# The first pass of a SwiGLU output product with eight fast pairs in place of six

## The chip, the cores and the metric

The kernel runs on one core of one Trainium2 chip. The metric is the device time of one execution in microseconds. All inputs are in device memory when it starts, and the output is written back there.

A core has TensorE (matrix products, into PSUM), VectorE ("DVE" in the profile), ScalarE ("ACT"), GpSimd ("POOL") and SyncE ("SP"), which here mostly issues transfers. Each runs its own list of instructions in order, and they wait for each other by semaphores.

## The reference

One layer of a decoder for 256 rows of 2048 columns, in float32:

```python
h = rms_norm(x, norm1_gain) * (1 + scale1) + shift1
x = x + gate1 * mixing_sublayer(h, ...)          # attention branches, w_out
h = rms_norm(x, norm2_gain) * (1 + scale2) + shift2
gate, up = jnp.split(h @ w_ffn_in, 2, axis=-1)   # 2048 -> 2 x 5632
x = x + gate2 * ((silu(gate) * up) @ w_ffn_out)  # 5632 -> 2048
```

The shift, scale and gate rows come from a product of silu(c) with w_ada. The change lies in the last product, (256 x 5632) @ (5632 x 2048).

## The kernel before

**Products in three parts.** TensorE multiplies a reduced float type (fp32r). So each factor is split in a high part (a cast on ScalarE) and a low part (VectorE subtracts the high part from the number), and `mm3` (L173 to L175) adds high x high, high x low and low x high: three matmuls of a 128 x 128 left factor with 512 weight columns. Weights come as 128 x 2 x 512 tiles ("raw"), transferred on SP's queue (L216), are cast (L236) and split (L222 in `sub`) into a hi and a lo tile, here called a room.

**The last product.** Its left factor is `act`, 11 units of 512 columns that the FFN before it made, each a hi and a lo tile. In chunks of 128 rows of the weights there are 44, so 22 pairs. It is done in two passes, over 1024 output columns each, by `fast_products`; pass one follows the order `OUT_A`, pass two `OUT_B`. An entry is a pair number and whether the pair is done by seven products.

**A pair.** The two chunks of a pair, the two column halves (512 each) and the two row tiles form a 2 x 2 by 2 x 2 block product. A plain pair takes eight `mm3`, 24 matmuls. A fast pair takes seven, 21 matmuls, by a scheme of Strassen's kind; it needs sums and differences of both factors. Those of the weights are made for every fast pair in `load_pair`: it splits r0 (1024 columns a partition), makes `ta` and `tb` (four subtractions of 512 columns in the rooms AR0 and A8, `OUT_TAGS`), and splits half of r1, `ta` and `tb`. The subtractions of all pairs of a pass are chained in their order (`chain`). Those of the left factor are made once for a unit, which is two pairs, in `sums_of_unit`: the sum of hi and lo (L1555) in AR0, four sums of 256 columns (L207) in A8, a cast (L1559) and the low part (L1560). Four units have them: 4, 5, 6 and 3 (`OUT_UNITS`), for the pairs 8 to 13, 6 and 7. A room given out by a tag belongs to one tile after the other in the order of the program: the next tile's writer waits for the last reader of the one before.

**Order of the work.** A planner lays out each engine's list. `load_pair` runs with raised priority, `LOOK` = 3 pairs ahead of the pair multiplied; the weights go round five rooms (four of a pool and X1 with X2) and, in pass one, six raw tiles (four and OD, KD); in pass two there are four. Other work fills in: at each position of the pass one step of the second gate row's sums is issued (`ada_mac`, L421; eight are left for this pass, each not before the split of the pair loaded last), and `hooks` names positions at which more is issued: the sums of units 4, 5 and 6 at positions 2, 4 and 6, the return of two column blocks of the residual at 15 and 16, and the gate row's finish at 19, 20 and 21 (`parts_of_gate2`, `rows_of_gate2`, L1577 to L1587), where position 21 also has the sums of the fourth unit, unit 3. After the last fast pair the four PSUM banks of shared products are put together (L312 to L316) and added into the output banks (`merge`, L272), for one row tile before position 20 and for the other before 21. Then `add_out` multiplies by the gate and adds to the residual (L1539, L1541).

In `OUT_A` before, positions 0 to 7 are plain, then fast pairs 8 to 13 alternate with plain pairs 14 to 19 (positions 8 to 19), and 20 and 21 are plain.

Of the kernel before, what the change touches and what calls it, by code (L numbers as in the profile page):

```python
# [11 lines left out]
F32R = mybir.dt.float32r  # L12
# [5 lines left out]
P = 128  # L18
# [27 lines left out]

FAST = range(2, 11)
OUT_UNITS = (4, 5, 6, 3)
OUT_A = tuple((p, 0) for p in range(8)) + tuple(x for i in range(6) for x in ((8 + i, 1), (14 + i, 0))) + ((20, 0), (21, 0))
OUT_B = ((0, 0), (1, 0)) + tuple(x for a, b in zip((8, 9, 10, 11, 12, 13, 6, 7), (2, 3, 4, 5, 14, 15, 16, 17)) for x in ((a, 1), (b, 0)))  # L50
PAIRS = ((0, 0), (1, 0), (5, 1), (2, 0), (6, 1), (7, 1), (3, 0), (4, 0))
PAIRS_4 = ((0, 0), (1, 0), (4, 1), (5, 1), (2, 0), (6, 1), (7, 1), (3, 0))
# [28 lines left out]
def trunk(ctx: ExitStack, tc: tile.TileContext, I, out):  # L81
# [12 lines left out]
    def nm(base):  # L94
        uid[0] += 1
        return f"{base}_{uid[0]}"

    def S(tag, shape, dtype=F32):
        return slot.tile(shape, dtype, tag=tag, name=nm(tag))
# [10 lines left out]
    def misc_bank(shape):  # L110
        return psm.tile(shape, F32, tag="misc", name=nm("misc"))
# [10 lines left out]
    state = {"rate": 0.0}  # L122
# [78 lines left out]
    def sums_of(sf, h, a, b):  # L201

        (a0, b0), (a1, b1) = ((x[:, a, :], x[:, b, :]) for x in h)
        for dst, x, y, op in (
            (0, a1, b1, ALU.add), (2, a0, a1, ALU.subtract), (1, sf[:, 0], a0, ALU.subtract), (3, b0, sf[:, 1], ALU.subtract)
        ):
            nc.vector.tensor_tensor(sf[:, dst], x, y, op=op)  # L207
# [1037 lines left out]
    for j in range(2):  # L1245
        hi = S(gtag[0][j], [P, 4, T], F32R)
        lo = S(gtag[1][j], [P, 4, T], F32R)
# [145 lines left out]
    def bring_back(n, tag):  # L1393
        x2[n] = S(tag, [P, NT, NB])
        nc.sync.dma_start(x2[n], x2_away[n])
# [87 lines left out]
    for i in range(NFF):  # L1483
# [30 lines left out]
        if ftags[2 * i] == ftags[2 * i + 1]:  # L1514
            hl = S(ftags[2 * i], [P, 2, 4, T], F32R)
            hi, lo = hl[:, 0], hl[:, 1]
        else:
            hi, lo = (S(tag, [P, 4, T], F32R) for tag in ftags[2 * i : 2 * i + 2])
# [17 lines left out]
    def add_out(n, t, ps, a=0, end=NB, base=0, store=True):  # L1536

        tmp = scr([P, end - a])
        nc.vector.tensor_mul(tmp, gate2[n][:, a:end], ps[:, a - base : end - base])  # L1539
        xr = x2[n][:, t, a:end]  # L1540
        nc.vector.tensor_add(xr, xr, tmp)  # L1541
        if store:
            nc.sync.dma_start(out[t * P : (t + 1) * P, n * NB + a : n * NB + end], xr)
# [7 lines left out]
    def sums_of_unit(n):  # L1551

        e = OUT_UNITS[n]
        full = S(OUT_TAGS[0], [P, 4, T])
        nc.vector.tensor_tensor(full, act[e][0].bitcast(F32), act[e][1].bitcast(F32), op=ALU.add)  # L1555
        sf = S(OUT_TAGS[1], [P, 4, 2, P])
        sums_of(sf, [full[:, :, t * P : (t + 1) * P] for t in range(NT)], slice(0, 4, 2), slice(1, 4, 2))
        hi, lo = (S(tag, [P, 4, 2, P], F32R) for tag in (("H2", "H3"), ("H4", "H5"), ("H6", "H7"), ("OD", "KD"))[n])
        nc.scalar.copy(hi, sf)  # L1559
        nc.vector.tensor_tensor(lo, sf, hi.bitcast(F32), op=ALU.subtract)  # L1560
        for m in range(2):
            out_sums[2 * e + m] = [(hi[:, j, m, :], lo[:, j, m, :]) for j in range(4)]


    state["more_rooms"] = (("X1", "X2"),)
    state["more_raws"] = ("OD", "KD")
    state["chain"] = None
    hooks = {at: (lambda n=n: sums_of_unit(n)) for n, at in enumerate((2, 4, 6))}
    state["rate"] = RATE_OUT
    ring["tags"] = ("OS1", "OS2")  # L1570
    bg.append(gate2_end())
# [3 lines left out]
    def parts_of_gate2(j):  # L1575
        hi, lo = (S(tag, [P, 2 * NB], F32R) for tag in OUT_TAGS)
        nc.scalar.copy(hi, state["gate2"][j])  # L1577
        nc.vector.tensor_tensor(lo, state["gate2"][j], hi.bitcast(F32), op=ALU.subtract)
        parts.append((hi, lo))

    def rows_of_gate2(j):
        for c in (slice(0, NB), slice(NB, 2 * NB)):
            ps = misc_bank([P, NB])
            with tc.issue_after(state["mm"].ins):
                for i, x in enumerate(parts[j]):
                    nc.tensor.matmul(ps, ones_r, x[:, c], start=i == 0, stop=i == 1)
            nc.scalar.copy(state["gate2"][j][:, c], ps)  # L1587

    def both(j):
        rows_of_gate2(j)  # L1590
        parts_of_gate2(j + 1)

    for n in range(2):
        hooks[15 + n] = lambda n=n: bring_back(n, ("OS1", "OS2")[n])
    behind = 1 + max(n for n, (_, fast) in enumerate(OUT_A) if fast)
    assert behind + 2 < len(OUT_A)
    hooks[behind] = lambda: parts_of_gate2(0)
    hooks[behind + 1] = lambda: both(0)
    hooks[behind + 2] = lambda: (rows_of_gate2(1), sums_of_unit(3))
    o = fast_products(w_fo, 0, NB, OUT_A, act_at, out_sums, acc_bank, misc_bank, OUT_TAGS, hooks)  # L1600
    gate2 = [a[:, c : c + NB] for a in state["gate2"] for c in (0, NB)]
    with prio():
        for n in range(2):
            for t in range(NT):
                add_out(n, t, o[n][t])
    state["more_raws"] = ()
    o = fast_products(w_fo, 2 * NB, 3 * NB, OUT_B, act_at, out_sums, misc_bank, acc_bank, OUT_TAGS, more=True)
    for n in (2, 3):
        bring_back(n, f"H{n}")
# [6 lines left out]
    n, pss = 3, o[1]  # L1616
# [42 lines left out]
```

## Time and profile before

| | |
|---|---|
| median of 3 runs | 1576.88 us (1576.4 to 1577.58) |
| the profiled execution | 1578.32 us |
| its span | 1576.5 us |
| matmuls on TensorE | 7186 |
| granted clock of TensorE | 1.000 |
| first pass of the last product on TensorE | 1339.58 to 1457.98 us of the span |

The profile has one execution. A span begins with the first instruction and ends with the last. "Busy" is the time in which an engine executes; a TensorE that is busy may still be paced by pipelining, so its starts are the better measure. In a timeline a line gives start, duration, engine, source line, operation, written and read tiles by name (numbers left out: AR for AR0, X for X0, X1 or X2), count, and in brackets idle time before it with what ended it. An instruction's duration overlaps the next by some 0.09 us on VectorE, so prices are taken from start to start.

### The profile page before, as it was taken

What the parts mean: (1) busy time and instruction counts of PE and PEld (TensorE: products, weight loads), DVE (VectorE), ACT (ScalarE), POOL (GpSimd) and SP (SyncE); (2) the same over time, 40 slices, a digit from 0 to 9 for tenths busy, and PEclk for the clock granted to TensorE, in tenths of its full rate; (3) what the DMA queues carried; (4) which work ended last, traced back from release to release, by engine and by line L of the source; (5) the groups of instructions that cost most, each with busy time, mean ns of one, the idle gap of its engine ahead of it and who ended that gap; (6) DMA issues with size and microseconds to landing.
All of it is one profiled execution on the core that took longest, in us unless ns stands there. A gap on an engine that the chain in (4) does not pass through costs nothing.

```text
span 1576.5 us, 20259 instructions
## 1 busy us (share of the span) xinstructions
PE 1563.9 (99%) x7186; PEld 1293.5 (82%) x7186; DVE 1394.4 (88%) x1704; ACT 876.0 (56%) x1215; POOL 12.3 (1%) x24
## 2 busy tenths in 40 slices
PE   8999999999999999999999999999999999999998
PEld 7878888888888788888888888888888888888887
DVE  6889996888889899987987888999999999899896
ACT  5654448875765545344444645556555555455553
POOL 1000000000000000000000000000000000000000
PEclk9999999999999999999999999999999999999999
DMA  9999987677787788879897886565566566876664
GB/s 333 362 325 322 333 309 239 216 240 228 236 294 262 259 268 298 298 260 317 305 328 256 299 305 216 187 213 188 200 202 212 174 201 235 287 228 201 222 208 140
DMA packets 196317, 402.26 MB, mean 255 GB/s; under 512 B 13102, under 2 KB 28116, under 8 KB 196216
## 3 DMA queue, kind: packets, MB, share of 16 engines
q1 hardware_dynamic: 194952, 397.75, 74.7%
q0 software_dynamic: 1088, 3.16, 0.5%
q8 instruction: 56, 0.92, 0.2%
q14 instruction: 45, 0.37, 0.1%
q10 hardware_dynamic: 176, 0.07, 0.0%
HBM read 395.68 MB, written 5.24 MB: 254 GB/s over the span
## 4 chain that ended last, share of the span: by engine, by line
PE 89%; DVE 4%; DMA 3%; ACT 2%; issue 1%; SPq 0%; ACTq 0%; DVEq 0%
PE acc L175 20%; PE acc L174 20%; PE acc L173 20%; PE misc L174 7%; PE misc L173 7%; PE misc L175 7%; DMA raw<-w_br_gla 1%; DVE wlo L222 1%; DVE wlo L166 1%; DMA T<-w_in 1%; PE acc L576 1%; PE misc L945 1%; DVE A L222 1%; DMA raw<-w_in 1%; ACT whi L165 1%
## 5 line engine op out<-in xcount | busy, mean ns | idle before, releaser
L165 ACT CAST whi<-raw 128x1024 fp32r<-128x1024 f32 (+1 forms) x277 | 278.8, 1012 | 290.6 <-PE acc L175 186.1
L166 DVE TENSOR_TENSOR wlo<-raw,whi 128x1024 fp32r<-128x1024 f32 (+1 forms) x277 | 321.8, 1171 | 94.4 <-ACT whi L165 93.3
L173 PE MATMUL acc<-whi,H 128*128 128x512 f32 x997 | 390.4, 392 | 1.0 <-ACT H L588 0.8
L174 PE MATMUL acc<-wlo,H 128*128 128x512 f32 x997 | 388.9, 390 | 0.8 <-DVE wlo L166 0.7
L175 PE MATMUL acc<-whi,H 128*128 128x512 f32 x997 | 388.8, 391 | 0.5 <-DVE H L595 0.4
L175 PEld LDWEIGHTS acc<-whi,H 128*128 128x128 f32 x997 | 187.0, 188 | 40.2 <-DVE H L595 1.4
L173 PEld LDWEIGHTS acc<-whi,H 128*128 128x128 f32 x997 | 187.2, 188 | 39.7 <-ACT H L588 1.3
L174 PEld LDWEIGHTS acc<-wlo,H 128*128 128x128 f32 x997 | 187.4, 188 | 39.1 <-DVE wlo L166 1.7
L236 ACT CAST whi<-raw 128x1024 fp32r<-128x1024 f32 (+1 forms) x130 | 125.4, 976 | 68.7 <-PE acc L175 31.8
L222 DVE TENSOR_TENSOR wlo<-raw,whi 128x1024 fp32r<-128x1024 f32 (+1 forms) x130 | 144.0, 1125 | 14.2 <-ACT whi L236 12.8
L175 PE MATMUL acc<-whi,A 128*128 128x512 f32 x221 | 86.1, 389 | 0.0
L174 PE MATMUL acc<-wlo,A 128*128 128x512 f32 x210 | 81.8, 390 | 0.4 <-DVE wlo L166 0.4
L173 PE MATMUL acc<-whi,A 128*128 128x512 f32 x210 | 82.0, 390 | 0.0
L174 PE MATMUL misc<-wlo,H 128*128 128x512 f32 (+1 forms) x190 | 73.6, 387 | 1.6 <-DVE wlo L222 1.6
L173 PE MATMUL misc<-whi,H 128*128 128x512 f32 (+1 forms) x190 | 73.6, 387 | 0.0
L175 PE MATMUL misc<-whi,H 128*128 128x512 f32 (+1 forms) x190 | 73.5, 387 | 0.0
L222 DVE TENSOR_TENSOR A<-raw,A 128x1024 fp32r<-128x1024 f32 (+2 forms) x54 | 53.9, 1002 | 0.8 <-ACT A L236 0.4
L421 DVE SCALAR_TENSOR_TENSOR ada<-AR,csil,ada 128x1024 f32<-128x1024 f32 x39 | 49.6, 1280 | 5.1 <-DMA AR<-w_ada 5.1
L175 PEld LDWEIGHTS acc<-whi,A 128*128 128x128 f32 x221 | 41.5, 188 | 8.6
L236 ACT CAST A<-raw 128x1024 fp32r<-128x1024 f32 (+1 forms) x36 | 35.9, 1003 | 20.4 <-PE acc L175 8.9
L174 PEld LDWEIGHTS acc<-wlo,A 128*128 128x128 f32 x210 | 39.4, 188 | 8.9 <-DVE wlo L166 0.8
L173 PEld LDWEIGHTS acc<-whi,A 128*128 128x128 f32 x210 | 39.4, 188 | 8.1
(682 smaller groups left out, 3039.0 us busy)
## 6 DMA issues: line engine op xcount, KB each, us to landing
raw<-w_in SPq DMA_DIRECT2D x192, 512.0 KB, 5.0
raw<-w_ffn_in SPq DMA_DIRECT2D x135, 512.0 KB, 4.5
raw<-w_ffn_out SPq DMA_DIRECT2D x73, 512.0 KB, 5.2
AR<-w_ada SPq DMA_DIRECT2D x62, 512.0 KB, 4.9
raw<-w_out SPq DMA_DIRECT2D x32, 512.0 KB, 5.1
OS<-w_ada SPq DMA_DIRECT2D x24, 512.0 KB, 5.9
KD<-w_ada SPq DMA_DIRECT2D x22, 512.0 KB, 5.1
AR<-w_ffn_in SPq DMA_DIRECT2D x22, 512.0 KB, 4.3
```

Source lines behind the costliest of these rows:

```text
L165: state["cast"] = nc.scalar.copy(hi[:, :n, :], raw[:, :n, :])
L166: state["split"] = nc.vector.tensor_tensor(lo[:, :n, :], raw[:, :n, :], hi[:, :n, :].bitcast(F32), op=ALU.subtract)
L173: nc.tensor.matmul(ps, lh, rh, start=start, stop=False, skip_group_check=seeded)
L174: nc.tensor.matmul(ps, lh, rl, start=False, stop=False, skip_group_check=seeded)
L175: state["mm"] = nc.tensor.matmul(ps, ll, rh, start=False, stop=stop, skip_group_check=seeded)
L222: done = nc.vector.tensor_tensor(dst, x, y, op=ALU.subtract)
L236: nc.scalar.copy(hi[:, :n, :], src)
L421: nc.vector.scalar_tensor_tensor(acc, raw, c, acc, op0=ALU.mult, op1=ALU.add)
L576: state["warm"] = nc.tensor.matmul(ps, ones_r, wide, start=True, stop=True)
L945: nc.tensor.matmul(ps[:n, t * N_GLA + h, :].rearrange("p (s l) -> p s l", l=L), at(f, h, t)[:, :n], odd(at(f, h, t)), start=True, stop=True,)
```

## The change

`OUT_A` gets eight fast pairs: positions 0 to 3 are plain pairs 0 to 3, then fast pairs 8 to 13, 6, 7 alternate with plain pairs 4, 5, 14 to 19 (positions 4 to 19, fast ones at the even positions), and 20 and 21 are as before. The sums of the four units are issued at positions 1, 5, 9 and 13; those of the fourth go to X0 and KD, so KD is no raw tile any more. The raw tile OD stays one in the second pass.

```diff
-OUT_A = tuple((p, 0) for p in range(8)) + tuple(x for i in range(6) for x in ((8 + i, 1), (14 + i, 0))) + ((20, 0), (21, 0))
+OUT_A = tuple((p, 0) for p in range(4)) + tuple(
+    x for a, b in zip((8, 9, 10, 11, 12, 13, 6, 7), (4, 5, 14, 15, 16, 17, 18, 19)) for x in ((a, 1), (b, 0))
+) + ((20, 0), (21, 0))
...
     def sums_of_unit(n):
...
-        hi, lo = (S(tag, [P, 4, 2, P], F32R) for tag in (("H2", "H3"), ("H4", "H5"), ("H6", "H7"), ("OD", "KD"))[n])
+        hi, lo = (S(tag, [P, 4, 2, P], F32R) for tag in (("H2", "H3"), ("H4", "H5"), ("H6", "H7"), ("X0", "KD"))[n])
...
-    state["more_raws"] = ("OD", "KD")
+    state["more_raws"] = ("OD",)
     state["chain"] = None
-    hooks = {at: (lambda n=n: sums_of_unit(n)) for n, at in enumerate((2, 4, 6))}
+    hooks = {at: (lambda n=n: sums_of_unit(n)) for n, at in enumerate((1, 5, 9, 13))}
...
-    hooks[behind + 2] = lambda: (rows_of_gate2(1), sums_of_unit(3))
+    hooks[behind + 2] = lambda: rows_of_gate2(1)
     o = fast_products(w_fo, 0, NB, OUT_A, act_at, out_sums, acc_bank, misc_bank, OUT_TAGS, hooks)
...
-    state["more_raws"] = ()
     o = fast_products(w_fo, 2 * NB, 3 * NB, OUT_B, act_at, out_sums, misc_bank, acc_bank, OUT_TAGS, more=True)
```

## The prediction

> **What bounds the kernel now.** I read the page first, then the last 240 us in windows, then VectorE's and TensorE's timelines there. The profiled execution took 1578.32 us, its span is 1576.5 us, so 1.8 us lie around it; it stands 1.4 us above the median of the runs, 1576.88 us. I work out a difference inside the span and add it to the median. 0.2%, about what a measurement of this kernel can tell from no change, is 3.15 us.
>
> ```profile
> span 1576.5 us, 20259 instructions
> PE 1563.9 (99%) x7186; PEld 1293.5 (82%) x7186; DVE 1394.4 (88%) x1704; ACT 876.0 (56%) x1215; POOL 12.3 (1%) x24
> ```
>
> ```profile
> 1360.00:1370.00 10.00, 10.00 (x46) 8.29 (x45) 7.68 (x7) 3.97 (x4) 0.00 (x0) 1.00 0.91 313
> ...
> 1400.00:1410.00 10.00, 10.00 (x46) 8.29 (x45) 9.80 (x13) 5.79 (x6) 0.00 (x0) 1.00 0.79 261
> 1410.00:1420.00 10.00, 10.00 (x45) 8.29 (x45) 8.85 (x11) 5.79 (x6) 0.00 (x0) 1.00 0.64 204
> ...
> 1510.00:1520.00 10.00, 10.00 (x46) 8.29 (x45) 9.15 (x11) 5.78 (x6) 0.00 (x0) 1.00 0.65 212
> ```
>
> The columns after the stretch are TensorE, weight loads, VectorE (DVE), ScalarE, GpSimd, granted clock, DMA share, GB/s. TensorE is fed without a hole; VectorE is close behind, at 9.80 us of 10 where seven-product and plain pairs alternate. So TensorE sets the time, but VectorE has little left.
>
> **What the change takes from TensorE.** TensorE's timeline gives starts:
>
> ```profile
> 1362.23 0.39 PE L173 MATMUL acc<-whi,A 128*128 128x512 f32 x1
> ...
> 1434.99 0.39 PE L173 MATMUL misc<-whi,T 128*128 128x512 f32 x1
> ...
> 1439.76 0.39 PE L173 MATMUL acc<-whi,AR 128*128 128x512 f32 x1
> ...
> 1445.20 0.39 PE L1586 MATMUL misc<-AR,ones_r 128*128 128x512 f32 x1
> ...
> 1446.13 0.39 PE L173 MATMUL acc<-X,H 128*128 128x512 f32 x1
> ```
>
> Position 18 of the pass, a pair by seven products, runs from 1434.99 to 1439.76: 4.77 us for 21 matmuls. Position 19, plain, runs to 1445.20: 5.44 us for 24. The change makes two more pairs fast: 2 x 0.67 = 1.34 us off TensorE. An alternation of both is 10.21 us. Position 4 starts at 1362.23, in the changed kernel too, since positions 0 to 3 are plain in both.
>
> **What it puts on VectorE.** One alternation, and what else runs there:
>
> ```profile
> 1415.92 1.22 DVE L222 TENSOR_TENSOR wlo<-KD,whi 128x1024 fp32r<-128x1024 f32 x1 [0.92 <-ACT whi L236]
> 1417.29 2.36 DVE L222 TENSOR_TENSOR wlo<-raw,whi 128x1024 fp32r<-128x1024 f32 x2
> 1419.57 0.68 DVE L222 TENSOR_TENSOR AR<-raw,raw 128x512 f32<-128x512 f32 x1
> 1420.17 0.68 DVE L222 TENSOR_TENSOR AR<-raw 128x512 f32<-128x512 f32 x1
> 1420.77 0.68 DVE L222 TENSOR_TENSOR wlo<-raw,whi 128x512 fp32r<-128x512 f32 x1
> 1421.37 0.68 DVE L222 TENSOR_TENSOR A<-raw,AR 128x512 f32<-128x512 f32 x1
> 1422.09 0.69 DVE L222 TENSOR_TENSOR A<-raw,A 128x512 f32<-128x512 f32 x1
> 1422.70 1.22 DVE L222 TENSOR_TENSOR X<-AR,X 128x1024 fp32r<-128x1024 f32 x1
> 1423.98 1.23 DVE L222 TENSOR_TENSOR wlo<-A,whi 128x1024 fp32r<-128x1024 f32 x1
> ```
>
> From start to start an instruction of 1024 columns takes 1.14 us (1417.29 to 1419.57 is two), one of 512 takes 0.60, and 0.12 more where it reads what the one before wrote (1421.37 to 1422.09). A plain pair is two of 1024: 2.28 us. A fast pair is three of 1024 and five of 512: 3.42 + 3.00 + 0.12 = 6.54 us. Together 8.82 us of TensorE's 10.21: 1.39 us to spare per alternation, seen above mostly as the 0.92 us wait.
>
> ```profile
> 1346.43 1.23 DVE L1555 TENSOR_TENSOR AR<-T,T 128x1024 f32<-128x1024 f32 x1
> ...
> 1352.18 1.28 DVE L421 SCALAR_TENSOR_TENSOR A<-OS,csil,A 128x1024 f32<-128x1024 f32 x1
> 1353.38 1.22 DVE L222 TENSOR_TENSOR wlo<-raw,whi 128x1024 fp32r<-128x1024 f32 x1
> ...
> 1357.85 0.42 DVE L207 TENSOR_TENSOR A<-AR,A 128x256 f32<-128x256 f32 x1
> 1358.18 1.22 DVE L222 TENSOR_TENSOR wlo<-raw,whi 128x1024 fp32r<-128x1024 f32 x1
> 1359.39 1.23 DVE L1560 TENSOR_TENSOR H<-A,H 128x1024 fp32r<-128x1024 f32 x1
> 1360.85 1.23 DVE L222 TENSOR_TENSOR wlo<-OD,whi 128x1024 fp32r<-128x1024 f32 x1 [0.23 <-ACT whi L236]
> 1361.99 1.28 DVE L421 SCALAR_TENSOR_TENSOR A<-OS,csil,A 128x1024 f32<-128x1024 f32 x1
> 1363.56 1.23 DVE L222 TENSOR_TENSOR X<-KD,X 128x1024 fp32r<-128x1024 f32 x1 [0.30 <-ACT X L236]
> ...
> 1366.28 1.23 DVE L222 TENSOR_TENSOR wlo<-raw,whi 128x1024 fp32r<-128x1024 f32 x1 [1.49 <-ACT whi L236]
> ...
> 1434.18 1.23 DVE L222 TENSOR_TENSOR wlo<-A,whi 128x1024 fp32r<-128x1024 f32 x1
> ...
> 1445.86 0.69 DVE L272 TENSOR_TENSOR acc<-acc,T 128x512 f32<-128x512 f32 x1
> 1446.46 0.69 DVE L272 TENSOR_TENSOR acc<-acc,KC 128x512 f32<-128x512 f32 x1
> ...
> 1452.50 1.23 DVE L1555 TENSOR_TENSOR AR<-A,A 128x1024 f32<-128x1024 f32 x1
> ```
>
> ```profile
> L421 DVE SCALAR_TENSOR_TENSOR A<-OS,csil,A 128x1024 f32<-128x1024 f32 x8 | 10.2, 1279 | 0.0
> ```
>
> A unit's sums are L1555, four L207 and L1560. L207 is 0.33 (1357.85 to 1358.18), so one unit costs 1.14 + 4 x 0.33 + 1.14 = 3.60 us. A step of the gate sum (L421) costs 1.20 (1352.18 to 1353.38); there are 8, and each follows the split of the pair loaded last, about one per position.
>
> Before, the sums of the first three units are over at 1360.5, beside plain pairs and TensorE's previous product, and the fourth runs after the pass (1452.50). After, only the first unit's come that early. Hooks 5, 9 and 13 lie inside the alternation, and there the sums share two rooms, AR0 and A8, with the differences of each fast pair, in the order of the program: the second unit's sums must wait until the pair at position 6 has been split, and the pair at position 8 cannot write AR0 before those sums have read it. All L222 of the pass are chained, so behind that first difference queue every later weight split, and behind these TensorE. The sums carry no raised priority, so gate steps that are ready go in between.
>
> The sum, from one fixed point. VectorE's instruction at 1360.85 fills the twelfth room of the pass; in the changed kernel the same room takes the last split of the first fast pair at the same time, because it comes free with TensorE's plain positions. The next room waits for TensorE's position 3 in both (1363.56). From there to the end of the first merge (L272 at 1445.86, finished by 1446.46) VectorE now has 82.9 us. TensorE goes on at 1446.13 with position 20, just as that merge ends: there is no slack at this place. After the change VectorE has, from 1363.56 to the same merge:
> - seven alternations (positions 5 to 18): 7 x 8.82 = 61.7
> - gate steps: two of 8 are done, six stay: 6 x 1.20 = 7.2
> - sums of three units: 3 x 3.60 = 10.8
> - what stands before between the last fast split's end (1434.18 + 1.14 = 1435.32) and the merge: 11.1
>
> That is 90.8 us in place of 82.9: the merge, and position 20 with it, comes 7.9 us later, even with VectorE never idle. TensorE's 1.34 us are inside this: it loses 9.2 us in waits and gains 1.34. For idle time under backlog I take what 1400 to 1410 left, 0.20 in 10 us, less the 0.12 already counted: 0.1 per 10 us over 91 us, 0.9 us. Together 8.8 us. Bounds: 7.9 with none, and 12.5 with half a microsecond in every 10.
>
> TensorE loses most of it before the merge. VectorE reaches the last split of position 16 at 1363.56 + 6 x 8.82 + 7.2 + 10.8 = 1434.5; TensorE would want it at 1362.23 + 6 x 10.21 + 3.4 (five of seven products) = 1426.9. So about 7.6 us go at positions 8, 10, 12 and 16, in pieces of up to 2.5 us, and the rest at position 20.
>
> **The smaller parts.** One buffer for raw weights fewer (five): the second pass runs before with four, and 1510 to 1520 shows TensorE with 46 matmuls all the same; nothing, up to 0.5 us where a late transfer meets the backlog. In the second pass it has five in place of four, and no wait of TensorE to shorten: nothing. The fourth unit's sums leave the seam, 3.6 us of VectorE where TensorE did not wait (1452.50): nothing, and they are the cover for a seam that is reached late. Room X0 is read last by the FFN's last unit, whose products end before position 0: no wait at hook 13. ScalarE gets four casts more and one moved, at 5.79 us of 10: hidden. The sums issue no transfer. The residual's columns are fetched back at positions 15 and 16 as before, on SP's queue, into rooms that the gate steps leave; later gate steps delay them, but they are needed only after the pass: nothing.
>
> [...] The windows put VectorE at 9.80 of 10 before the change adds to it. [...]
>
> **Rivals.**
> - VectorE keeps up (the other side). If the sums are taken early, by readiness and not in the rooms' program order, they fall into idle time before 1361 as now. Then 90.8 - 10.8 = 80.0 us stand against 82.9 - 1.34 = 81.6, TensorE never waits, and the time is 1575.5 us. It decides at 1.6 us of sums after 1363.56. Against it: VectorE idles 1.49 us before 1366.28 with both rooms free, and the fourth unit's sums, whose factors were long there, still start only at 1452.50, in program order. 6%.
> - Only some sums slip in early. One unit less is 5.2 us later (1582.1), two are 1.6 (1578.5). 10%.
> - The waits are longer and bring down TensorE's clock, or sums come behind two pairs. A single wait of 4 us in place of 2.5 at three hooks adds 4.5 us; 15 matmuls at half speed (0.227 us each now, 4.77 / 21) add 3.4 us. 1589 to 1594. The clock reads 1.00 in each window, but no window here holds such a wait. 10%. [...]
> - That the change does not do what it says: its eight pairs and their factors are all written out in the order, so I give this nothing.
>
> **How the numbers follow.** VectorE last, as summed: 74%, 1576.88 + 8.8 = 1585.7 us, itself from 1584 to 1589.5. The range: above, its bound of 12.5 us gives 1589.4, and part of the clock's case reaches in, so 1590; below, the case of two units early, 1578.5, is mostly left out: 1579. Slower by over 0.2% (above 1580.0): 74 + 10 + some 2 of the middle case = 86%. Within: 13%, the middle case's rest and the gain of 1.34 us, which is under 3.15. Faster by over 0.2% would need more than TensorE saves: 1%.
>
> **What would show it.** Right: in TensorE's waits of the first pass new rows on L222 and L1560, some 9 us; VectorE above 9.7 of 10 from 1365 to 1455; L1555 three times among fast pairs; the merge's L272 at about 1454.6; six matmuls fewer. Wrong: no wait of TensorE, or sums before 1361, or VectorE idle while TensorE waits for weights in transit.

## The result, and the profile after

The changed kernel takes 1587.91 us (median of 4 runs, 1586.27 to 1589.92), the kernel before, beside it on the same chip, 1577.12 us: 10.8 us more, a ratio of 1.0065 (95% interval 1.0053 to 1.0078). The profiled execution after took 1586.27 us, below that median; its span is 8.0 us longer than before's. The page's head and totals:

```profile
span 1584.5 us, 20270 instructions
...
PE 1569.1 (99%) x7180; PEld 1293.6 (82%) x7180; DVE 1402.6 (89%) x1716; ACT 877.4 (55%) x1219; POOL 12.5 (1%) x24
```

Six matmuls went, and TensorE is "busy" 5 us longer all the same. On TensorE the second pass begins at 1465.95 us in place of 1457.98 and is as long as before. Both kernels have the same 6144 matmuls ahead of the first pass, and the execution after reaches the next one at 1337.90 us, 1.7 us earlier than the one before (1339.58). So the first pass itself is 9.7 us longer, 128.06 us in place of 118.40. Its windows, columns as in the prediction:

```profile
1380.00:1390.00 10.00, 7.84 (x32) 5.55 (x32) 9.81 (x13) 6.52 (x7) 0.00 (x0) 1.00 0.53 168
1390.00:1400.00 10.00, 10.00 (x45) 8.06 (x44) 10.00 (x12) 5.47 (x6) 0.00 (x0) 1.00 0.80 236
1400.00:1410.00 10.00, 8.42 (x32) 5.99 (x31) 9.61 (x13) 2.94 (x3) 0.00 (x0) 0.92 0.68 231
1410.00:1420.00 10.00, 9.23 (x32) 6.89 (x32) 9.93 (x13) 4.62 (x5) 0.00 (x0) 0.74 0.68 204
1420.00:1430.00 10.00, 10.00 (x46) 8.28 (x45) 8.89 (x12) 5.29 (x6) 0.00 (x0) 1.00 0.66 207
1430.00:1440.00 10.00, 9.46 (x40) 7.02 (x39) 9.14 (x10) 5.87 (x7) 0.00 (x0) 1.00 0.42 135
```

In four of these windows TensorE is idle, for 2.16, 1.58, 0.77 and 0.54 us, 5.05 in all; VectorE is busy for 9.81, 9.61, 9.93 and 9.14 us of them. In two windows the granted clock is below 1. TensorE's timeline (in brackets the idle time and what ended it) has the waits:

```profile
1383.75 0.50 PE L177 MATMUL acc<-whi,H 128*128 128x512 f32 x1
1386.35 0.50 PE L175 MATMUL misc<-whi,H 128*128 128x512 f32 x1 [2.10 <-ACT whi L238]
...
1407.21 0.51 PE L175 MATMUL acc<-X,ada 128*128 128x512 f32 x1 [1.14 <-ACT X L238]
...
1411.96 0.80 PE L175 MATMUL misc<-whi,H 128*128 128x512 f32 x1 [0.77 <-ACT whi L238]
1412.55 0.63 PE L176 MATMUL misc<-wlo,H 128*128 128x512 f32 x1
1412.98 0.63 PE L177 MATMUL misc<-whi,H 128*128 128x512 f32 x1
```

They name ScalarE's cast (L238). Before the waits of 2.10 and 0.77 us the cast had waited itself for VectorE's differences. Before the wait of 1.14 us it had not: it waited for TensorE to leave the room that it writes, as ScalarE's timeline shows.

```profile
1406.12 1.04 ACT L238 CAST X<-raw 128x1024 fp32r<-128x1024 f32 x1 [6.42 <-PE acc L177]
```

So these 1.14 us are a chain from TensorE over ScalarE back to TensorE, in the order that the planner gave. Another 0.44 us behind them go to the cast of the sums (L1561), the next on ScalarE. The last two starts above are 0.43 us apart instead of 0.227: windows of 1 us put the clock at 0.50 from 1408.4 to 1415.2. Some 14 matmuls lost 0.2 us each, 2.8 us. VectorE's timeline ahead of the first wait, and at the places of the other sums and the merge (all lines are 2 further down than before):

```profile
1376.75 1.22 DVE L1557 TENSOR_TENSOR AR<-T,T 128x1024 f32<-128x1024 f32 x1
1377.88 1.28 DVE L423 SCALAR_TENSOR_TENSOR A<-OS,csil,A 128x1024 f32<-128x1024 f32 x1
1379.08 0.75 DVE L209 TENSOR_TENSOR A<-AR 128x256 f32<-128x256 f32 x2
...
1380.66 0.69 DVE L224 TENSOR_TENSOR AR<-raw,raw 128x512 f32<-128x512 f32 x1
...
1382.47 1.22 DVE L1562 TENSOR_TENSOR H<-A,H 128x1024 fp32r<-128x1024 f32 x1
...
1403.16 1.22 DVE L1557 TENSOR_TENSOR AR<-T,T 128x1024 f32<-128x1024 f32 x1
...
1420.88 1.23 DVE L1557 TENSOR_TENSOR AR<-A,A 128x1024 f32<-128x1024 f32 x1
...
1455.33 0.69 DVE L274 TENSOR_TENSOR acc<-acc,T 128x512 f32<-128x512 f32 x1
```

The second unit's sums and a gate step stand before the fast pair's first difference (1380.66), as the prediction had them; the third and fourth unit's sums follow at 1403 and 1420.

5.05 us idle and 2.8 us by the clock, less the 1.34 that two more fast pairs save, are 6.5 of the pass's 9.7 us. The other 3.1 us lie mostly beside the waits, some 1 us at each of the three places (1382 to 1387, 1405 to 1418, 1430 to 1447), where starts are further apart than 0.227 us without an idle time that the profile lists.

### The profile page after: what moved, and what is told of

Read it like the earlier page. It is cut to its first block, busy times and chain, and to the rows that moved or that the text cites. A ratio compares the mean times of both kernels' runs of the same rounds, so it can differ in the third digit from the quotient of the medians.

```text
span 1584.5 us, 20270 instructions
## 1 busy us (share of the span) xinstructions
PE 1569.1 (99%) x7180; PEld 1293.6 (82%) x7180; DVE 1402.6 (89%) x1716; ACT 877.4 (55%) x1219; POOL 12.5 (1%) x24
## 4 chain that ended last, share of the span: by engine, by line
PE 87%; DVE 6%; ACT 2%; DMA 2%; issue 2%; SPq 0%; ACTq 0%; DVEq 0%
PE acc L177 20%; PE acc L176 20%; PE acc L175 20%; PE misc L176 7%; PE misc L177 7%; PE misc L175 7%; PE acc L578 1%; DVE wlo L168 1%; DVE wlo L224 1%; PE misc L947 1%; DVE A L224 1%; DMA AR<-w_ada 1%; DVE T L423 1%; DMA raw<-w_br_gla 0%; PE misc L571 0%
## 5 line engine op out<-in xcount | busy, mean ns | idle before, releaser
L238 ACT CAST whi<-raw 128x1024 fp32r<-128x1024 f32 (+1 forms) x130 | 124.5, 975 | 57.1 <-PE acc L177 15.4
L177 PE MATMUL acc<-whi,A 128*128 128x512 f32 x209 | 81.4, 390 | 0.0
L175 PE MATMUL acc<-whi,A 128*128 128x512 f32 x198 | 77.3, 391 | 0.0
L176 PE MATMUL acc<-wlo,A 128*128 128x512 f32 x198 | 77.2, 390 | 0.0
L238 ACT CAST whi<-OD 128x1024 fp32r<-128x1024 f32 (+1 forms) x34 | 34.1, 1002 | 32.9 <-DVE OD L224 14.5
L238 ACT CAST A<-raw 128x1024 fp32r<-128x1024 f32 (+1 forms) x36 | 35.9, 1003 | 20.5 <-PE acc L177 8.9
L177 PEld LDWEIGHTS acc<-whi,A 128*128 128x128 f32 x209 | 39.2, 188 | 8.1
L175 PEld LDWEIGHTS misc<-whi,H 128*128 128x128 f32 x190 | 35.9, 190 | 11.6 <-ACT whi L238 4.5
```

What stands on the lines that cost most here:

```text
L175: nc.tensor.matmul(ps, lh, rh, start=start, stop=False, skip_group_check=seeded)
L176: nc.tensor.matmul(ps, lh, rl, start=False, stop=False, skip_group_check=seeded)
L177: state["mm"] = nc.tensor.matmul(ps, ll, rh, start=False, stop=stop, skip_group_check=seeded)
L238: nc.scalar.copy(hi[:, :n, :], src)
```

## The experiments

Theories: **amount** (the prediction's: VectorE's total work up to the merge decides), **rooms** (AR0 and A8 in program order block the differences), **peaks** (what counts is where VectorE falls behind), and the smaller suspects, raw buffers and clock. Where a run's first pass is compared below, it is that of the profiled execution, counted by matmuls as above; it was 118.40 us before, and 118.37 and 118.43 in the two variants of the kernel before that should not change it (one raw buffer fewer, no gate steps). The kernel before ran beside each kernel on the same chip: 1577.43 us beside the runs with sums early, rooms held back and no gate steps; 1577.49 beside those with no late set, moved sums, own rooms and GpSimd; 1577.48 beside one and two late sets; 1578.02 beside the last two.

**All sums early.**

```diff
-    hooks = {at: (lambda n=n: sums_of_unit(n)) for n, at in enumerate((1, 5, 9, 13))}
+    hooks = {at: (lambda n=n: sums_of_unit(n)) for n, at in enumerate((0, 1, 2))}
...
+    hooks[2] = lambda: (sums_of_unit(2), sums_of_unit(3))
```

> The changed kernel with the sums of all four units issued at positions 0, 1 and 2 (two units at 2), before the first fast pair writes AR0; nothing else changes. Theory V (VectorE's work between 1363.56 and the merge decides): 10.8 us of sums leave that stretch, 80.0 us stand against 81.6, TensorE waits under 1 us in the pass, the granted clock stays at 1.000, 1575.5 to 1577.5 us. Theory R (the sums hold the rooms AR0 and A8 and so stop the chain of weight splits; the amount of work does not matter): the same, 1575.5 to 1577.5. Theory D (one raw buffer fewer): no change from the changed kernel, 1586 to 1589.

Measured: 1583.36 us, ratio 1.0034 (1.0021 to 1.0046), outside every theory's range. A window, VectorE's and TensorE's timelines of this kernel:

```profile
1350.00:1360.00 10.00, 10.00 (x46) 8.29 (x45) 9.93 (x13) 3.36 (x4) 0.00 (x0) 1.00 0.59 197
```

```profile
1362.28 0.69 DVE L224 TENSOR_TENSOR AR<-OD,raw 128x512 f32<-128x512 f32 x1
...
1364.09 1.22 DVE L1562 TENSOR_TENSOR KD<-A,X 128x1024 fp32r<-128x1024 f32 x1
```

```profile
1367.89 0.50 PE L175 MATMUL misc<-whi,H 128*128 128x512 f32 x1 [1.66 <-ACT whi L238]
```

The four sets all but fill VectorE before 1362, the first fast pair's differences come only then, and TensorE waits at position 4; behind the wait the clock reads 0.50 for 3.4 us. The sums did not vanish into free time: with the first fast pair at position 4, that time belongs to its weights.

**Rooms of their own, held back and not held.** Sums in KC and X0; once issued after the last split, once free.

```diff
-        full = S(OUT_TAGS[0], [P, 4, T])
-        nc.vector.tensor_tensor(full, ...)
-        sf = S(OUT_TAGS[1], [P, 4, 2, P])
+        full = S((OUT_TAGS[0], "KC", "KC", "KC")[n], [P, 4, T])
+        with tc.issue_after(state["split"].ins) if n else nullcontext():   # held back; without this line: free
+            nc.vector.tensor_tensor(full, ...)
+        sf = S((OUT_TAGS[1], "X0", "X0", OUT_TAGS[1])[n], [P, 4, 2, P])
```

> The changed kernel with the sums of units two to four in rooms that the fast pairs do not use (KC, and X0 for two of them), but each held back behind the last weight split of its position, so that they stay in the alternation. The same VectorE instructions in the same stretch, without the blocking. Theory V: VectorE's total until the merge is as before the edit, 1583 to 1589 us, TensorE's waits move but stay near 9 us. Theory R: the chain no longer waits for sums, 1576 to 1579. Theory D: 1586 to 1589.

Measured, held back: 1594.64 us, ratio 1.0095 (1.0079 to 1.0111); slower than the change itself, and above the range of both theories. VectorE's timeline, and a wait in TensorE's:

```profile
1384.76 1.22 DVE L1558 TENSOR_TENSOR KC<-T,T 128x1024 f32<-128x1024 f32 x1
...
1387.64 0.42 DVE L209 TENSOR_TENSOR X<-KC 128x256 f32<-128x256 f32 x1
...
1391.38 0.42 DVE L209 TENSOR_TENSOR X<-KC 128x256 f32<-128x256 f32 x1
...
1397.12 1.22 DVE L1563 TENSOR_TENSOR H<-X,H 128x1024 fp32r<-128x1024 f32 x1
```

```profile
1395.03 0.50 PE L175 MATMUL acc<-whi,H 128*128 128x512 f32 x1 [0.21 <-ACT H L1562]
```

Nothing blocks the differences now, but the set is scattered between splits over 13.6 us (1384.76 to 1398.3) and TensorE waits for the factor as well. Rooms of their own do not save the loss by themselves. The run does not compare amounts cleanly, since holding the sets back also stretched them out.

> The changed kernel with its second to fourth unit's sums in rooms of their own (KC, X0; the fourth's second room stays A8) and not held back, so that the planner may place them where VectorE is free; the order shows the second and third unit's sums ahead of the second fast pair, the fourth's first addition early and the rest late. VectorE theory: 14.4 us of sums over the idle time before 1362 (some 9 us from 1330) and the 10.1 us after it, neither enough alone: loss between that of all sums early (5.9 us) and none, 1579 to 1583. Rival (only the moment at which a sum is in the way counts, and nothing is in the way where the planner chooses): 1575.5 to 1577.5.

Measured, not held: 1582.09 us, ratio 1.0034 (1.0022 to 1.0046), inside the amount theory's range. The clock stays at 1.00 and TensorE's listed waits are 2.3 us in all, none over 0.64.

**The gate row's steps taken out of the pass** (the change, and its partner, the kernel before with the same edit).

```diff
-GATE2_CUT = 12
+GATE2_CUT = 16
```

> The changed kernel without gate steps in the pass: all sixteen rows of the second gate are summed in the stage of the product with w_out, none is left for the last product. To be read against the kernel before with the same edit (next run), since eight more steps there may cost. Theory V: 7.2 us of VectorE leave the stretch; 83.6 against 82.9 and 0.9 us of idle time: 1 to 3 us slower than its partner, where the change itself was 10.8. Theory R: the sums still hold the rooms: 8 to 11 us slower than its partner. Theory D: 8 to 11.

> The kernel before without gate steps in the pass, partner of the run above. All theories: TensorE did not wait in this pass, so nothing is won there; eight steps of 1.2 us more in the stage of the product with w_out cost nothing to 10 us: 1576 to 1587.

Measured: 1591.91 us (ratio 1.0087, 1.0073 to 1.0100) and 1588.34 (1.0065, 1.0053 to 1.0078). Done earlier, the eight steps cost 10.9 us where they went, so neither kernel is of use, but between the two the change costs 3.6 us in place of 10.8, a little above the forecast of 1 to 3. In the first pass alone the two are 1.4 us apart. With 9.6 us (8 x 1.20) less for VectorE in the pass most of the loss is gone. That speaks for amount, and against rooms, which were as before; fewer steps beside the sums also make the peaks lower, so it does not tell amount from peaks.

**The late sums left out, one set after the other.** A left-out unit's pairs take an earlier unit's factors.

```diff
         e = OUT_UNITS[n]
+        if n > k:                    # k = 0, 1, 2: no, one, two late sets
+            for m in range(2):
+                out_sums[2 * e + m] = out_sums[2 * OUT_UNITS[k] + m]
+            return
```

> The changed kernel, but the sums of the second, third and fourth unit are left out: their fast pairs multiply with the first unit's factors, so 3 x 3.60 = 10.8 us of VectorE's work is gone and the order of pairs, the eight fast pairs and the five raw buffers stay. VectorE theory (the amount of VectorE's work in the pass decides): 90.8 - 10.8 = 80.0 us stand against TensorE's 81.6, no wait of TensorE in the pass, 1575.5 to 1577.5 us. Rival (the order of pairs, the fewer raw buffers or the fast pairs themselves cost the time): at least half of the 10.8 us stays, 1582 to 1588.

> The changed kernel with the sums of the third and fourth unit left out (their pairs multiply with the second unit's factors): one set of late sums, 3.6 us of VectorE, stays, at hook 5. Ledger of the prediction (what exceeds VectorE's room counts in full): 1578.5 us. Rival, equal shares: each set costs a third of the 11.8 us that lie between no late set (1576.1) and three (1587.9), so 1580.0. Rival, by the hook: each costs the 1.9 us that each of two late sets cost the kernel before, less nothing more, so 1577.5 to 1578.2.

> The changed kernel with the fourth unit's sums alone left out (its pairs multiply with the third unit's factors): two late sets, 7.2 us of VectorE, at hooks 5 and 9. Ledger of the prediction: 1582.1 us. Rival, equal shares: 1584.0. Rival, by the hook: 1579.5 to 1580.2, and then the third set alone would cost some 8 us, more than twice its VectorE time, which would point to the halved clock at 1409 to 1415 as a cost of its own.

| late sets | the ledger of the prediction | measured | ratio to before (interval) | first pass against 118.40 | of that, matmuls at half clock |
|---|---|---|---|---|---|
| 0 | 1575.5 | 1576.12 | 0.9996 (0.9988 to 1.0005) | -1.2 | 0 |
| 1 | 1578.5 | 1581.75 | 1.0024 (1.0014 to 1.0034) | +5.3 | 14 x 0.2 = 2.8 |
| 2 | 1582.1 | 1586.91 | 1.0060 (1.0048 to 1.0073) | +10.2 | 20 x 0.2 = 4.0 |
| 3 (the change) | 1585.7 | 1587.91 | 1.0065 (1.0053 to 1.0078) | +9.7 | 14 x 0.2 = 2.8 |

Without late sums, eight fast pairs and five raw buffers cost nothing, and TensorE has no wait in the pass. So the whole loss comes with the late sets. But it does not grow as the ledger has it: the first set costs 5.6 us, the second 5.2, the third 1.0 (each difference is uncertain by 2 to 3 us). Equal shares (1580.0 and 1584.0) fit one set and are too low for two; a price by the hook is too low for both.

Much of the ledger's miss is the clock, which it leaves out. The last two columns are of one execution each. Without the half clock the pass is 2.5, 6.2 and 6.9 us longer with one, two and three sets, where the ledger has 1.6, 5.2 and 8.8. The kernel with one late set, TensorE's timeline, then VectorE's:

```profile
1386.23 0.79 PE L175 MATMUL misc<-whi,H 128*128 128x512 f32 x1 [2.10 <-ACT whi L238]
1386.82 0.63 PE L176 MATMUL misc<-X,H 128*128 128x512 f32 x1
1387.25 0.63 PE L177 MATMUL misc<-X,H 128*128 128x512 f32 x1
```

```profile
1410.76 1.22 DVE L224 TENSOR_TENSOR wlo<-A,whi 128x1024 fp32r<-128x1024 f32 x1 [3.44 <-ACT whi L238]
```

The one set makes the same 2.10 us wait as in the change, and here the clock falls within it (1385.5). Later VectorE has caught up and idles 3.44 us. ScalarE's timeline says why:

```profile
1408.73 1.05 ACT L238 CAST X<-raw 128x1024 fp32r<-128x1024 f32 x1 [4.39 <-PE acc L177]
1409.69 1.04 ACT L238 CAST whi<-A 128x1024 fp32r<-128x1024 f32 x1
```

The first cast waits for TensorE, which is late, to leave a room; the cast that VectorE needs stands behind it. What TensorE lost at 1386 is not given back, however free VectorE is afterwards. So a total that takes VectorE as never idle is not what decides at one set, and that the ledger comes within 1 us of the pass without the half clock is luck. By three sets VectorE hardly idles any more (3.1 us from 1370 to 1450), and its total comes near. I read this as the peaks theory for the first sets and amount for the whole; the next run tests it with the clock at 1.00.

**The sums moved into the alternation of the kernel before.**

```diff
-    hooks = {at: (lambda n=n: sums_of_unit(n)) for n, at in enumerate((2, 4, 6))}
+    hooks = {at: (lambda n=n: sums_of_unit(n)) for n, at in enumerate((2, 9, 13))}
```

> The kernel before with the sums of its second and third unit moved from hooks 4 and 6 to 9 and 13, inside the alternation; six fast pairs and six raw buffers as before. VectorE theory: 7.2 us of work move into a stretch (1360 to 1450) whose windows left VectorE 10.1 us idle, in pieces, so 0 to 3 us: 1577 to 1580. Rival (whatever sums stand between a fast pair's differences delay the splits behind them by their whole 3.6 us, however much idle time there is elsewhere): 1581 to 1585.

Measured: 1581.30 us, ratio 1.0023 (1.0013 to 1.0033), at the lower edge of the rival's range and above the amount theory's. TensorE's waits in the pass:

```profile
PE misc L173 <- ACT whi L236: 2.7, 2, 1.3
```

(Total, times, longest.) Two waits of 1.3 us, one behind each moved set, in a kernel with no wait before, though VectorE's idle time was enough in sum. The clock stays at 1.00, and the first pass is 3.4 us longer: this is the price of the waits alone. In these runs no late set was free where a fast pair's six and a half microseconds stood close behind it.

**The sums on GpSimd.** As the run with rooms of their own, not held; additions, differences and low part of the late sets issued on GpSimd.

```diff
+        eng = nc.gpsimd if n else nc.vector
...
-            nc.vector.tensor_tensor(full, ...)
+            eng.tensor_tensor(full, ...)
...
-        sums_of(sf, ...)
+        sums_of(sf, ..., eng)
...
-        nc.vector.tensor_tensor(lo, ...)
+        eng.tensor_tensor(lo, ...)
```

> As the run with own rooms, but the additions and subtractions of the second to fourth unit's sums run on GpSimd, which is busy 1% of the span; VectorE loses 10.8 us of work. GpSimd's nearest row is a 1024-column cast of 1.144 us, so a unit takes 3.6 us or some times that. VectorE theory: as with the sums left out, 80.0 us against 81.6, so 1575.5 to 1578, if the factors are ready by their pairs. Rival (GpSimd is much slower, so the factors come late, or its accesses slow VectorE's instructions beside it): 1580 to 1590, with VectorE's 1024-column rows above 1.23 us or TensorE waiting for GpSimd.

Measured: 1592.34 us, ratio 1.0094 (1.0080 to 1.0108). GpSimd's timeline, then VectorE's, then ScalarE's:

```profile
1342.65 2.40 POOL L1559 TENSOR_TENSOR KC<-T,T 128x1024 f32<-128x1024 f32 x1 [387.08 <-DVE misc L274]
...
1362.12 3.35 POOL L1564 TENSOR_TENSOR H<-X,H 128x1024 fp32r<-128x1024 f32 x1
```

```profile
1343.22 2.91 DVE L1564 TENSOR_TENSOR H<-A,H 128x1024 fp32r<-128x1024 f32 x1
...
1363.16 3.38 DVE L423 SCALAR_TENSOR_TENSOR A<-OS,csil,A 128x1024 f32<-128x1024 f32 x1
```

```profile
1350.94 1.05 ACT L1563 CAST H<-X 128x1024 fp32r<-128x1024 f32 x1 [6.14 <-POOL X L209]
```

Two costs show in the rows. Beside GpSimd, VectorE's 1.23 and 1.28 us instructions took 2.91 and 3.38; and ScalarE, in order, sat 6.14 us at the cast of the sums with the weights' casts queued behind it. TensorE waits for both, 2.76 us at the longest, and the clock reads 0.50 for 6.8 us from 1361.9. What makes VectorE's instructions longer beside GpSimd was not shown.

**An order with the fast pairs later.**

```diff
+OUT_A = tuple((p, 0) for p in range(6)) + (
+    (8, 1), (14, 0), (9, 1), (15, 0), (10, 1), (11, 1), (16, 0), (12, 1), (13, 1), (17, 0), (6, 1), (18, 0), (7, 1)
+) + ((19, 0), (20, 0), (21, 0))
...
-    hooks = {at: (lambda n=n: sums_of_unit(n)) for n, at in enumerate((1, 5, 9, 13))}
+    hooks = {at: (lambda n=n: sums_of_unit(n)) for n, at in enumerate((0, 2, 4, 12))}
```

> Eight fast pairs as in the change, but six plain positions ahead of them in place of four, the first three units' sums at hooks 0, 2 and 4, beside those plain positions as before, and only the fourth unit's at hook 12; in return two fast pairs stand next to each other three times. It asks whether any order of these pairs beats both kernels. Totals theory (the ledger): two fast pairs more and the fourth set are 2 x 4.26 + 3.60 = 12.1 us of VectorE against the 10.1 us that 1360 to 1450 left idle before, so 2 us over: 1577.5 to 1580. Peaks theory (what counts is where VectorE falls behind, because TensorE's loss there is not given back, and the halved clock that follows a stall): two fast pairs in a row need 13.1 us of VectorE in 9.5 us of TensorE, stalls at those places, 1581 to 1587.

Measured: 1584.68 us, ratio 1.0040 (1.0028 to 1.0053), as the peaks theory had it. (There are two doubles, not the three that the expectation counts.) TensorE's timeline in the second:

```profile
1417.24 0.50 PE L176 MATMUL acc<-wlo,H 128*128 128x512 f32 x1 [1.49 <-DVE wlo L224]
...
1420.91 0.80 PE L175 MATMUL misc<-whi,H 128*128 128x512 f32 x1 [2.46 <-ACT whi L238]
```

These two waits stand in the second pair of the double 12 and 13, next to the late set; a third, 1.33 us at 1401.38, stands in the second pair of the double 10 and 11, with no set near. The clock reads 0.50 for 6.8 us from 1420.3. No version beat the kernel before, and the run without late sums says how much there was to win: 1.4 us, which these runs cannot tell from nothing.

**One raw buffer fewer in the kernel before.**

```diff
-    state["more_raws"] = ("OD", "KD")
+    state["more_raws"] = ("OD",)
```

> The kernel before with one buffer for raw weights fewer in the first pass (five, as in the change), nothing else. The prediction gave this part nothing, up to 0.5 us: 1577 to 1578. Rival (transfers come too late with five): 1579 to 1583.

Measured: 1578.35 us against 1578.02, ratio 0.9997 (0.9988 to 1.0006): nothing, and TensorE has no wait in the pass.

## Why the prediction was right, and where it was not

The forecast of 1585.7 us, 8.8 more than before, stands 2 us under the 10.8 measured, and 1587.91 lies in its range. Its mechanism, VectorE late in the first pass, is shown by the run without late sums, by the pair without gate steps and by TensorE's waits. That the number came so near is in part luck, as the points on the pieces and the clock say. Point by point:

- **TensorE's saving of 1.34 us**: in the run without late sums the first pass is 117.24 us, 1.16 less than before. Near it, and too small for the timing of whole runs to resolve.
- **The ledger's end**: the merge was forecast at 1454.6 and came at 1455.33, but in an execution that was 1.7 us ahead at the start of the pass (position 4 begins at 1360.55, not at 1362.23). Against that start it is 11.2 us later than before, where the ledger has 8.8. Its term for idle time was mis-sized: 0.9 us, where the windows from 1370 to 1450 leave VectorE idle for 3.1 us.
- **The step that failed** is that a sum over the whole pass tells the price. At three late sets it comes near, but it gives 1578.5 and 1582.1 for one and two where 1581.75 and 1586.91 were measured; of these misses the half clock is some 2.8 and 4 us. With the clock at 1.00 the moved sets show the step: 7.2 us of work go into 10.1 us of idle time, the sum gives no loss, and the pass is 3.4 us longer. The step left out that VectorE can work ahead only as far as rooms are free, so that later free time did not repay an earlier wait. The number of rooms was not varied, so that this limit is the reason rests on the casts that waited for TensorE to leave a room.
- **"Pieces of up to 2.5 us" at positions 8, 10, 12 and 16**: the longest is 2.10, they lie at positions 8, 12 and 16, none at 10, and their sum is 5.05 us in place of 7.6. Of these, 1.14 us were spent on a cast that had waited for TensorE, not for VectorE. The rest was to come at position 20 as a wait for the merge. There is none: in the changed kernel VectorE's merge is 9.5 us late and the second pass 8.0; TensorE's row for 1440 to 1470 is busy throughout.
- **The clock** was left out of the forecast's sum and given to a rival with waits of 4 us. In the changed kernel it stayed at 1.00 over the wait of 2.10 us and fell behind waits of 1.14 and 0.44 us. That cost some 2.8 us, about what the idle time came short by (2.55): here two errors offset each other. The 3.1 us beside the waits had no term in the forecast either. The rival's 15 matmuls at half speed, 3.4 us, were the author's estimate and rest on no row of before, whose clock reads 1.000; in the changed kernel some 14 lost 0.2 us each (0.43 between starts in place of 0.227).
- **Rooms in program order**: the order came as described, but with rooms of their own the sums cost 4.6 us or, held back, 17.2. The rooms count by where they put the sets: freed, the planner places them earlier and 6 of the 10.8 us go; held back among the splits, rooms of their own save nothing.
- **The first rival's condition** (sums before 1361 and then 1575.5 us) was wrong by 7.9 us: its ledger, 80.0 against 81.6, began at 1363.56 and took the stretch before as free.
- **The smaller parts**: raw buffers, second pass and seam at nothing were right (0.9997; the second pass starts 7.97 us and ends 8.0 us late).
- **What would show it**: three sets among fast pairs and six matmuls fewer, yes; VectorE above 9.7 throughout, no (8.89 and 9.14 between 1420 and 1440); waits on L222 and L1560, mostly no: the profile names ScalarE's cast, which stood behind VectorE in two of the three long waits.

## What to carry to other kernels

Work added to the second-busiest engine is to be weighed stretch by stretch against how far that engine can run ahead: where the bound engine has no slack, as here, a wait is not repaid by free time later in the stage. Here a total over the stage came near the price only when the added work filled the stage; for less, look at the longest run of work between two deliveries. Where the bound engine is TensorE, allow for its clock beside each wait: in the change the half clock cost some 2.8 us, where the longest wait is 2.10. Taking work to an idle engine helps only if the busy engine's instructions do not grow longer beside it (here 3.38 us in place of 1.28) and no engine that works in order sits waiting for its results (here 6.14 us).

## What the runs showed of the hardware

One stall, three clocks. Three kernels are alike up to a wait of 2.10 us that ends at 1386.2 to 1386.4 (2.11 us in the third). The windows behind it, of the change, of one late set and of two:

```profile
1388.00:1389.00 1.00, 1.00 (x6) 0.80 (x5) 1.00 (x2) 1.00 (x2) 0.00 (x0) 1.00 0.95 367
...
1391.00:1392.00 1.00, 1.00 (x6) 0.81 (x6) 1.00 (x2) 0.00 (x0) 0.00 (x0) 1.00 0.73 254
```

```profile
1388.00:1389.00 1.00, 1.00 (x4) 0.71 (x4) 1.00 (x2) 1.00 (x3) 0.00 (x0) 0.50 0.89 328
...
1391.00:1392.00 1.00, 1.00 (x4) 0.71 (x3) 1.00 (x3) 0.00 (x0) 0.00 (x0) 0.50 0.90 270
```

```profile
1388.00:1389.00 1.00, 1.00 (x3) 0.77 (x3) 1.00 (x2) 1.00 (x3) 0.00 (x0) 0.50 0.95 363
...
1391.00:1392.00 1.00, 1.00 (x6) 0.82 (x5) 1.00 (x3) 0.00 (x0) 0.00 (x0) 1.00 0.81 264
```

The clock column reads 1.00 throughout, 0.50 for 6.8 us (from 1385.5), and 0.50 for 3.4 us (from 1387.2). So a wait of 2.1 us came with the half clock in two of the three kernels and without it in one; what decides that was not shown. With two late sets the clock is at 0.50 a second time, for 6.8 us from 1411.06. The four executions of the change, 1586.27 to 1589.92 us with clocks of 0.996 to 0.999, do not sort by the clock.
